# Sliding windows by DMA alone: 11 of 32 batches staged in SBUF and stored twice, the rest copied HBM to HBM, on two rings

## The chip, the core and the metric

The kernel runs on one core of one Trainium2 chip. The metric is the device time of one execution in microseconds (us). Data lives in HBM, the chip's main memory; SBUF is the core's on-chip memory of 128 partitions. Copies are made by 16 DMA engines. A DMA is issued by the queue of an engine: SP (`nc.sync`) or ACT (`nc.scalar`); each of the two has a hardware ring of its own. A DMA is broken into packets, one for each contiguous run of memory.

## The reference: what is computed

Nothing is computed; overlapping windows are copied. The input is fp32 of shape (32, 4096, 256), the output (32, 127, 64, 256).

```python
window_size = 64
stride = 32
n_windows = (length - window_size) // stride + 1      # 127
for i in range(n_windows):
    start = i * stride
    result[:, i] = x[:, start:start + window_size].copy()
```

A window is 64 rows of 256 floats, 65,536 bytes, and contiguous both in the input and in the output. Windows advance by half a window. Call 32 rows (32,768 bytes) a block: a batch has 128 blocks, and window i is blocks i and i + 1. So every block but the first and the last of a batch is written twice. The input has 134.2 MB, the output 266.3 MB.

## The kernel before

The file holds five strategies; line 8 picks `"d2d"`, and only `_d2d` (line 33) and `_d2d_batch` (line 14) run. `_SbufBatch`, `_sbuf`, `_mix`, `_pair` and `_hybrid` are not used, and SBUF holds no data.

`_d2d` loops over the 32 batches. `D2D_NQ` is 1 (line 30), so all DMAs are issued on `nc.sync`. For each batch `_d2d_batch` issues two DMAs from HBM to HBM at line 26: one of 112 windows (`D2D_CHUNK`, line 11) and one of the remaining 15. Both sides of each are rows of 65,536 bytes, one for each window; the rows of the source overlap by half. There are 64 DMAs in all. No DMA depends on another; the Tile framework hands each a semaphore and lets the queue wait for an older one where semaphores run out. The order of the work is the order of issue, batch after batch. In the profile, line 283 is the start of the program, line 297 its end.

Of the kernel before, what the change touches and what calls it, by code (L numbers as in the profile page):

```python
# [7 lines left out]
STRATEGY = "d2d"  # L8
NSB = 7

D2D_CHUNK = 112


def _d2d_batch(q, x, out_flat, b, L, D, W, S, n_win):
    win_elems = W * D
    step_elems = S * D
    w0 = 0
    while w0 < n_win:
        nw = min(D2D_CHUNK, n_win - w0)
        src = bass.AP(  # L20
            x.tensor,
            x.offset + (b * L + w0 * S) * D,
            [[step_elems, nw], [1, win_elems]],
        )
        dst = out_flat[b * n_win + w0 : b * n_win + w0 + nw]
        q.dma_start(out=dst, in_=src, max_dma_last_dim=65536)
        w0 += nw


D2D_NQ = 1  # L30


def _d2d(nc, x, out, B, L, D, W, S, n_win):
    out_flat = out.rearrange("b i w d -> (b i) (w d)")
    queues = [nc.sync, nc.scalar][:D2D_NQ]
    for b in range(B):
        _d2d_batch(queues[b % len(queues)], x, out_flat, b, L, D, W, S, n_win)


class _SbufBatch:  # L40

    def __init__(self, tc, ctx, x, out, B, L, D, W, S, n_win, bufs=3):
        assert W % S == 0 and L % S == 0
        self.m = W // S
        self.n_blocks = L // S
        assert self.n_blocks <= 128
        self.blk = S * D
        self.n_win = n_win
        self.x_blocks = x.rearrange("b (n s) d -> b n (s d)", n=self.n_blocks)
        self.out_rows = out.rearrange("b i w d -> b i (w d)")  # L50
        self.pool = ctx.enter_context(tc.tile_pool(name="swin_sbuf", bufs=bufs))
        self.dtype = x.dtype
        self.chunks = []
        w0 = 0
        for cnt in (64, 48, 16, 15):
            while n_win - w0 >= cnt or (w0 < n_win and cnt == 15):
                cnt_eff = min(cnt, n_win - w0)
                self.chunks.append((w0, cnt_eff))
                w0 += cnt_eff
        assert sum(c for _, c in self.chunks) == n_win  # L60

    def alloc(self):
        return self.pool.tile([self.n_blocks, self.blk], self.dtype, name="xb")

    def load(self, q, t, b):
        q.dma_start(out=t[:, :], in_=self.x_blocks[b])

    def stores(self, q, t, b):
        for k in range(self.m):
            for (w0, cnt) in self.chunks:  # L70
                src = t[w0 + k : w0 + k + cnt]
                dst = self.out_rows[b, w0 : w0 + cnt, k * self.blk : (k + 1) * self.blk]
                q.dma_start(out=dst, in_=src, max_dma_last_dim=65536)


def _sbuf(ctx, tc, nc, x, out, B, L, D, W, S, n_win):
    sb = _SbufBatch(tc, ctx, x, out, B, L, D, W, S, n_win, bufs=4)
    queues = [nc.sync, nc.scalar]
    tiles = {}
    for b in range(B):  # L80
        t = sb.alloc()
        tiles[b] = t
        sb.load(queues[b % 2], t, b)
        if b >= 1:
            sb.stores(queues[(b - 1) % 2], tiles[b - 1], b - 1)
            del tiles[b - 1]
    sb.stores(queues[(B - 1) % 2], tiles[B - 1], B - 1)


def _mix(ctx, tc, nc, x, out, B, L, D, W, S, n_win, nsb=None, lookahead=2):  # L90
    if nsb is None:
        nsb = NSB
    out_flat = out.rearrange("b i w d -> (b i) (w d)")
    sb = _SbufBatch(tc, ctx, x, out, B, L, D, W, S, n_win, bufs=4)
    queues = [nc.sync, nc.scalar]

    span = B - 4
    sbuf_set = set()
    if nsb > 0:
        for j in range(nsb):  # L100
            sbuf_set.add(1 + j * span // nsb)
    assert len(sbuf_set) == nsb

    def flush_stores(qidx):
        t, bb = pending.pop(0)
        j = 0
        for (w0, cnt) in sb.chunks:
            for k in range(sb.m):
                q = queues[(qidx + j) % 2]
                src = t[w0 + k : w0 + k + cnt]  # L110
                dst = sb.out_rows[bb, w0 : w0 + cnt, k * sb.blk : (k + 1) * sb.blk]
                q.dma_start(out=dst, in_=src, max_dma_last_dim=65536)
                j += 1

    pending = []
    n_d2d_left = B - nsb
    for b in range(B):
        q = queues[b % 2]
        if b in sbuf_set:
            t = sb.alloc()  # L120
            sb.load(q, t, b)
            pending.append((t, b))
            if len(pending) > lookahead:
                flush_stores(b % 2)
        else:
            _d2d_batch(q, x, out_flat, b, L, D, W, S, n_win)
            n_d2d_left -= 1
            if pending and n_d2d_left < 2 * len(pending):
                flush_stores(b % 2)
    qi = 0  # L130
    while pending:
        flush_stores(qi)
        qi += 1


def _pair(ctx, tc, nc, x, out, B, L, D, W, S, n_win, nsb=None):
    if nsb is None:
        nsb = NSB
    assert 3 * nsb + 4 <= B - nsb, "not enough d2d batches to pair"
    out_flat = out.rearrange("b i w d -> (b i) (w d)")  # L140
    sb = _SbufBatch(tc, ctx, x, out, B, L, D, W, S, n_win, bufs=4)
    queues = [nc.sync, nc.scalar]
    blk = sb.blk

    sbuf_batches = [4 * g for g in range(nsb)]
    d2d_batches = [b for b in range(B) if b not in set(sbuf_batches)]
    di = 0

    W_CHUNKS = [(0, 64), (64, 48), (112, 15)]
    L_CHUNKS = [(0, 64), (64, 48), (112, 16)]  # L150

    def d2d_chunk(q, b, w0, cnt):
        src = bass.AP(
            x.tensor,
            x.offset + (b * L + w0 * S) * D,
            [[S * D, cnt], [1, W * D]],
        )
        q.dma_start(
            out=out_flat[b * n_win + w0 : b * n_win + w0 + cnt],
            in_=src,  # L160
            max_dma_last_dim=65536,
        )

    def load_part(q, t, b, p0, cnt):
        q.dma_start(out=t[p0 : p0 + cnt], in_=sb.x_blocks[b, p0 : p0 + cnt])

    def store_part(q, t, b, w0, cnt, k):
        src = t[w0 + k : w0 + k + cnt]
        dst = sb.out_rows[b, w0 : w0 + cnt, k * blk : (k + 1) * blk]
        q.dma_start(out=dst, in_=src, max_dma_last_dim=65536)  # L170

    tiles = {}
    n_groups = nsb + 2
    for g in range(n_groups):
        qa = queues[g % 2]
        qb = queues[1 - g % 2]
        a_instrs = []
        if g < nsb:
            bload = sbuf_batches[g]
            t = sb.alloc()  # L180
            tiles[bload] = t
            for (p0, cnt) in L_CHUNKS:
                a_instrs.append(("load", t, bload, p0, cnt, None))
        if g >= 2:
            bst = sbuf_batches[g - 2]
            ts = tiles.pop(bst)
            for (w0, cnt) in W_CHUNKS:
                for k in range(sb.m):
                    a_instrs.append(("store", ts, bst, w0, cnt, k))
        b_needed = [ins[4] for ins in a_instrs]  # L190
        b_instrs = []
        nb_d2d = 3 if g < nsb else 2
        for _ in range(nb_d2d):
            bd = d2d_batches[di]
            di += 1
            for (w0, cnt) in W_CHUNKS:
                b_instrs.append((bd, w0, cnt))
        n = max(len(a_instrs), len(b_instrs))
        for i in range(n):
            if i < len(a_instrs):  # L200
                ins = a_instrs[i]
                if ins[0] == "load":
                    load_part(qa, ins[1], ins[2], ins[3], ins[4])
                else:
                    store_part(qa, ins[1], ins[2], ins[3], ins[4], ins[5])
            if i < len(b_instrs):
                bd, w0, cnt = b_instrs[i]
                d2d_chunk(qb, bd, w0, cnt)
    rem = d2d_batches[di:]
    for j, bd in enumerate(rem):  # L210
        for (w0, cnt) in W_CHUNKS:
            d2d_chunk(queues[j % 2], bd, w0, cnt)


def _hybrid(ctx, tc, nc, x, out, B, L, D, W, S, n_win):
    out_flat = out.rearrange("b i w d -> (b i) (w d)")
    sb = _SbufBatch(tc, ctx, x, out, B, L, D, W, S, n_win, bufs=3)

    sbuf_batches = [b for b in range(B) if (b + 1) * NSB // B > b * NSB // B]
# [16 lines left out]
    if pending is not None:  # L236
        sb.stores(q_sb, pending[0], pending[1])
# [64 lines left out]
```

## Time and profile before

| | |
|---|---|
| time, median of 2 runs | 807.83 us (807.09 to 808.56) |
| span of the profiled execution | 805.2 us |
| instructions | 109, of which 64 issue DMAs |
| bytes moved by DMA | 266.34 MB, mean 331 GB/s |
| HBM read and written | 266.34 MB each |
| one DMA, from issue to landing, median | 100.5 us |

The profiled execution's own time is its span; the three numbers of the first row come from other, unprofiled executions. In the page, section 2 cuts the span into 40 slices; its DMA row is the mean busy share of the 16 engines in tenths, and GB/s what they moved. A byte copied from HBM to HBM counts once in the GB/s of the engines, and twice in the HBM traffic (read and written). Section 3 gives the packets of each queue. The view by stretches gives, for a window of time, its length, the busy time of POOL, the clock, the DMA share and the GB/s; the share times 16 is the number of engines at work on average. The view of the waits of a queue gives for each line what it waited for: total us, times, longest.

### The profile page before, as it was taken

How to read it: one execution, taken by the hardware profiler on the slowest of the kernel's cores; microseconds unless marked ns; L12 is line 12 of the kernel's file. 1: busy time of each engine (PE TensorE's matmuls, PEld its weight loads, DVE VectorE, ACT ScalarE, POOL GpSimd, SP SyncE). 2: the span in 40 equal slices, each digit the busy share in tenths (PEclk: the TensorE clock that was granted, in tenths of full speed). 3: DMA queues.
4: the chain of work that ended last, by engine and by line, in shares of the span. 5: the costliest groups of instructions: out<-in, count | busy, mean ns of one | idle time of the engine just before them, and what ended most of it. 6: DMA issues, size and time to landing. Idle time of an engine off the chain costs nothing. (4 is left out here: it accounts for less than half of the span.)

```text
span 805.2 us, 109 instructions
## 1 busy us (share of the span) xinstructions
POOL 0.2 (0%) x4
## 2 busy tenths in 40 slices
POOL 0000000000000000000000000000000000000000
DMA  9999999999999999999999999999999999999995
GB/s 313 355 322 332 342 316 352 322 339 335 319 358 313 322 352 319 348 329 335 339 316 358 319 329 348 313 361 319 335 335 332 342 322 339 332 322 332 326 335 254
DMA packets 5056, 266.34 MB, mean 331 GB/s; under 512 B 992, under 2 KB 992, under 8 KB 992
## 3 DMA queue, kind: packets, MB, share of 16 engines
q1 hardware_dynamic: 5056, 266.34, 98.3%
HBM read 266.34 MB, written 266.34 MB: 662 GB/s over the span
## 5 line engine op out<-in xcount | busy, mean ns | idle before, releaser
L283 POOL MEMSET const-bfloat16-1.0<- 128x1 bf16 x1 | 0.1, 101 | 0.0
L283 POOL MEMSET const-uint8-127<- 128x1 uint8 x1 | 0.1, 101 | 0.0
L283 POOL MEMSET const-float32-0.0<- 128x1 f32 x1 | 0.1, 98 | 0.2 <-issue 0.2
L283 POOL MEMSET const-float32-1.0<- 128x1 f32 x1 | 0.1, 98 | 0.0
## 6 DMA issues: line engine op xcount, KB each, us to landing
out_dram<-in_x_dram SPq DMA_DIRECT2D x64, 100.5
```

Of the source, the lines that this page charges most:

```text
L283: nc = _bacc.Bacc("TRN2", target_bir_lowering=False, num_devices=1)
```

## The change

The five strategies go, and a class `Copier` with four kinds of DMA comes. 11 batches (1, 4, 7, ... 31) are staged: `load` brings a whole batch, 128 blocks, into an SBUF tile, one block for each partition, and four `store` calls write it out: blocks 0 to 126 as the first halves of the windows (`half` 0), blocks 1 to 127 as the second halves, each in a part of 112 rows and one of 15. The other 21 batches go from HBM to HBM: `d2d` for 112 windows as before, and `d2d_fine` for the last 15, whose rows are cut into 16 runs of 4096 bytes, with the 16 as the outer dimension.

Work goes in 11 groups. Group g stages one batch on one ring (`qa`) and copies two direct batches on the other (`qb`); the rings change roles from group to group. The load of a batch is issued two groups ahead, on the ring that will store it; the pool has four tiles. The last group has one direct batch left. There are 97 DMAs: 11 loads, 44 stores, 21 of `d2d` and 21 of `d2d_fine`.

```diff
-STRATEGY = "d2d"
-NSB = 7
...
+class Copier:
...
+    def d2d(self, q, b, w0, n):
+        blk = self.blk
         q.dma_start(
+            out=self.oap((b * self.nw + w0) * 2 * blk, [[2 * blk, n], [1, 2 * blk]]),
+            in_=self.xap(b * self.nb + w0, [[blk, n], [1, 2 * blk]]),
             max_dma_last_dim=65536,
         )
+    def d2d_fine(self, q, b, w0, n, parts=16):
+        blk = self.blk
+        e = 2 * blk // parts
+        q.dma_start(
+            out=self.oap((b * self.nw + w0) * 2 * blk, [[e, parts], [2 * blk, n], [1, e]]),
+            in_=self.xap(b * self.nb + w0, [[e, parts], [blk, n], [1, e]]),
+        )
+    def load(self, q, t, b):
+        q.dma_start(
+            out=t[:, :], in_=self.xap(b * self.nb, [[self.blk, self.nb], [1, self.blk]])
+        )
+    def store(self, q, t, b, half, p0, n):
+        blk = self.blk
+        w = b * self.nw + p0 - half
+        q.dma_start(
+            out=self.oap(w * 2 * blk + half * blk, [[2 * blk, n], [1, blk]]),
+            in_=t[p0 : p0 + n, :],
+        )
...
-    if STRATEGY == "d2d":
-        _d2d(nc, x, out, B, L, D, W, S, n_win)
...
+    c = Copier(nc, x, out, B, L, D, W, S, n_win)
+    pool = ctx.enter_context(tc.tile_pool(name="xb", bufs=4))
+    rings = [nc.sync, nc.scalar]
+    staged = list(range(1, B, 3))
+    direct = [b for b in range(B) if b not in staged]
+    tiles = {}
+    def load(q, g):
+        if g < len(staged):
+            tiles[g] = pool.tile([128, c.blk], x.dtype, name="xb")
+            c.load(q, tiles[g], staged[g])
+    load(rings[0], 0)
+    load(rings[1], 1)
+    for g, b in enumerate(staged):
+        qa, qb = rings[g % 2], rings[1 - g % 2]
+        load(qa, g + 2)
+        t = tiles.pop(g)
+        for half in (0, 1):
+            if direct:
+                d = direct.pop(0)
+                c.d2d(qb, d, 0, 112)
+                c.d2d_fine(qb, d, 112, 15)
+            c.store(qa, t, b, half, half, 112)
+            c.store(qa, t, b, half, 112 + half, 15)
+    for d in direct:
+        c.d2d(rings[d % 2], d, 0, 112)
+        c.d2d_fine(rings[d % 2], d, 112, 15)
```

`xap` and `oap`, left out above, make an access pattern on the input and the output from a start and a list of [step, count]; `blk` is 8192 elements, `nb` 128, `nw` 127.

More of the change, by code (lines that the diff above doesn't have):

```diff
@@ L4 @@
 import concourse.tile as tile
-from concourse import bass_utils, mybir
+from concourse import mybir
 from concourse._compat import with_exitstack
-STRATEGY = "d2d"
-NSB = 7
[L11 to L27, printed above, removed]
@@ L30 @@
[L30 to L46, printed above, removed]
-        self.blk = S * D
[L48 to L73, printed above, removed]
@@ L76, in _sbuf @@
[L76 to L133, printed above, removed]
@@ L136, in _pair @@
[L136 to L157, printed above, removed]
+BLK = 32 * 256
@@ new lines, with __init__, xap, oap @@
+class Copier:
+    def __init__(self, nc, x, out, B, L, D, W, S, n_win):
+        assert W == 2 * S and L % S == 0
+        self.nc, self.x, self.out = nc, x, out
+        self.blk = S * D
+        self.nb = L // S
+        self.nw = n_win
+    def xap(self, block, dims):
+        return bass.AP(self.x.tensor, self.x.offset + block * self.blk, dims)
+    def oap(self, elem, dims):
+        return bass.AP(self.out.tensor, self.out.offset + elem, dims)
+    def d2d(self, q, b, w0, n):
+        blk = self.blk
@@ L158, in d2d_chunk @@
         q.dma_start(
-            out=out_flat[b * n_win + w0 : b * n_win + w0 + cnt],
-            in_=src,
+            out=self.oap((b * self.nw + w0) * 2 * blk, [[2 * blk, n], [1, 2 * blk]]),
+            in_=self.xap(b * self.nb + w0, [[blk, n], [1, 2 * blk]]),
             max_dma_last_dim=65536,
         )
[L164 to L219, printed above, removed]
-    d2d_batches = [b for b in range(B) if b not in set(sbuf_batches)]
-    q_d2d = nc.sync
-    q_sb = nc.scalar
-    pending = None
-    prefetch = None
-    for b in range(B):
-        if b in set(d2d_batches):
-            _d2d_batch(q_d2d, x, out_flat, b, L, D, W, S, n_win)
-        else:
-            t = sb.alloc()
-            sb.load(q_sb, t, b)
-            if pending is not None:
-                sb.stores(q_sb, pending[0], pending[1])
-            pending = (t, b)
-    if pending is not None:
-        sb.stores(q_sb, pending[0], pending[1])
+    def d2d_fine(self, q, b, w0, n, parts=16):
[5 more added lines that the diff above has]
+        )
@@ L249 @@
     nc = tc.nc
-    W = int(window_size)
-    S = int(stride)
+    W, S = int(window_size), int(stride)
     B, L, D = x.shape
     n_win = (L - W) // S + 1
-    assert out.shape == (B, n_win, W, D), (out.shape, (B, n_win, W, D))
-    if STRATEGY == "d2d":
-        _d2d(nc, x, out, B, L, D, W, S, n_win)
-    elif STRATEGY == "sbuf":
-        _sbuf(ctx, tc, nc, x, out, B, L, D, W, S, n_win)
-    elif STRATEGY == "mix":
-        _mix(ctx, tc, nc, x, out, B, L, D, W, S, n_win)
-    elif STRATEGY == "pair":
-        _pair(ctx, tc, nc, x, out, B, L, D, W, S, n_win)
-    else:
-        _hybrid(ctx, tc, nc, x, out, B, L, D, W, S, n_win)
+    assert out.shape == (B, n_win, W, D)
+    c = Copier(nc, x, out, B, L, D, W, S, n_win)
[24 more added lines that the diff above has]
+        c.d2d_fine(rings[d % 2], d, 112, 15)
 _INS = ['x', 'window_size', 'stride']
```

## The prediction

> **What bounds the kernel now.** I read the page first. Compute does nothing (POOL 0.2 us in all), so the chain of work that ended last says nothing here, and the DMA rows carry the case.
>
> ```profile
> DMA  9999999999999999999999999999999999999995
> DMA packets 5056, 266.34 MB, mean 331 GB/s; under 512 B 992, under 2 KB 992, under 8 KB 992
> q1 hardware_dynamic: 5056, 266.34, 98.3%
> HBM read 266.34 MB, written 266.34 MB: 662 GB/s over the span
> ```
>
> The 16 DMA engines are busy 98.3% of the span. 5056 less 992 is 4064 packets, one of 65,536 B for each window (32 x 127). The 992 small ones are 32 x (16 + 15): a DMA of 112 windows signs off on 16 engines, one of 15 windows on 15. Every byte crosses HBM twice, once read and once written.
>
> Next, the waits of the SP queue and the issuing line, to see if the issuer starves the engines.
>
> ```profile
> SPq L26 <- DMA out_dram<-in_x_dram: 662.8, 56, 21.6
> ```
> ```profile
> L26 SPq DMA_DIRECT2D out_dram<-in_x_dram x64: 528/748/927, 0.7 to 707.6; - x64
> DMA to landing us min/median/max: 24.6/100.5/101.9
> ```
>
> SP issues 64 DMAs at a median of 748 ns and waits 56 times: all but the first eight wait for an older one, so at most eight are in flight. A DMA lands 100.5 us after its issue, mostly queued behind others. The last is issued at 707.6 us. The issuer is far ahead and bounds nothing.
>
> Busy engines are not yet a bound: they may be held up together. The view of busy time by stretch decides (DMA share and GB/s are the last two columns).
>
> ```profile
> 20.00:700.00 680.00, 0.00 (x0) 1.00 1.00 334
> 745.00:780.00 35.00, 0.00 (x0) 1.00 0.94 331
> 790.00:800.00 10.00, 0.00 (x0) 1.00 0.73 315
> ```
>
> With all 16 busy they move 334 GB/s, 20.9 each (3.14 us per packet). At 0.94, some 15 engines move 331, 22.0 each. At 0.73, 11.7 engines move 315, 27.0 each (2.43 us per packet). A quarter of the engines gone costs 6% of the rate. So an engine alone can do at least 27.0, together 16 x 27.0 = 432 GB/s, and something shared stops direct copies at about 334. The likeliest shared thing is HBM traffic, 2 x 334 = 668 GB/s of reads and writes.
>
> **The change, part by part.** All sums are against the profiled execution: span 805.2 us, 2.6 below the median of the two runs (807.83), which I add at the end. At 334 GB/s the 266.34 MB take 797.4 us; the other 7.8 us are the start and the thinning end.
>
> *Traffic.* A batch has 8.32 MB of output and 4.19 MB of input. Direct, the engines move 8.32 MB and HBM carries 16.65. Staged, the engines move 4.19 in and 8.32 out, 12.52 MB, and HBM carries the same 12.52. With 11 staged and 21 direct: engine bytes 266.34 + 11 x 4.19 = 312.5 MB (+17%); HBM traffic 532.7 - 11 x 4.13 = 487.3 MB (-8.5%), all of it fewer reads: 220.9 read, 266.3 written. It trades the scarce resource, if that is total HBM traffic, against one with slack.
>
> *Bounds.* If both ceilings were used perfectly: engines 312.5 / 432 = 723 us, HBM 487.3 / 668 = 729 us. The sum cannot be below 729 by these rows. If the kinds never helped each other, direct at 334 and staged at 432 one after the other: 174.8 / 334 + 137.7 / 432 = 523 + 319 = 842 us. Alone, a staged batch is dearer than a direct one (29.0 us against 24.9). The whole gain is that direct packets run faster beside staged ones. That is why both rings matter: in each group one ring carries staged work and the other two direct batches.
>
> *How they mix.* The trace has one ring, so how engines share two is not in it. I bound by two ways. (a) Equal bytes: 129.3 MB staged beside 129.3 direct; HBM would allow 668 / 1.5 = 445, engines stop at 432: 599 us. The two first loads, 8.4 MB alone, 19 us. The direct rest, 45.5 MB at 334, 136 us. Sum 754. (b) Packet by packet, 64 KB direct against 32 KB staged: 2 to 1 in bytes, so HBM stops the pair at 668 / (5/3) = 401 GB/s. 10.5 pairs of 8.32 + 16.65 MB, 262.2 MB, take 654 us; the remaining 50.3 MB staged face staged work or nothing at 432, 116 us. Sum 770. I take the middle, 762, since neither is shown.
>
> [...]
>
> *Staged packets.* No row shows a packet with an end in SBUF. Its rate lies between that of a direct packet under full load, 20.9 GB/s, and 27.0, the fastest engine shown (a faster one is possible, but HBM then binds). I take 27.0: the staged packet burdens HBM half as much, as the uncrowded engines of 790 to 800 us do. The lower end is a rival below.
>
> [...]
>
> *Packets.* Per engine the packets go from 316 to 823: 147 of 64 KB, 315 of 4 KB (the fine form of the 15-window tails), 88 loads, 176 stores, 97 sign-offs. The engine time outside packets is 1.7%, 13.7 us for 316, so at most 43 ns each; 507 more cost 0 to 22 us. I take 0, because the stretch from 20 to 700 us shows a share of 1.00: one packet's gap is covered by the next. The other ring is the cover; without it, 22.
> The fine form puts 15 windows on 16 engines evenly. The 15-row stores still use 15 engines, 22 packets of 32 KB less on one, 0.2% of the bytes. Worth 0 to 5 us of the 7.8 at the ends; I take nothing.
>
> *Issue and waits.* 97 DMAs (11 loads, 44 stores, 42 direct) over two queues at 0.75 us: some 37 us per queue, beside transfers. SP no longer issues alone; ACT, idle before, issues half. New waits: a load waits until the tile of four groups earlier is stored; behind it on its ring stand the four stores of its group. Those older stores left on the same ring two groups before, with 16.6 MB of direct work since (about 40 us), so they should be done. A store waits for a load issued two groups earlier. If a ring does stall, the other still feeds all 16 engines at 334 or more instead of 401, 1.7 us lost per 10 us. If the limit of eight in flight is shared by both rings, that is still nearly one group (26 MB, 65 us of work). I take 0; ten such stalls of 10 us would be 17.
> *Crowding.* In (b) engines run at 401 of 432 while HBM is full. The row at 0.94 lost 1% near such a corner; 0 to 3%, up to 20 us. Taken as 0.
>
> Sum: 762 + 7.8 + 2.6 = 773 us.
>
> **The rivals.**
> *Writes bind, not the total.* Reads and writes fell together in every row, so a limit of 334 on writes alone fits too. Writes stay 266.3 MB: 797 us, plus 19 for the two opening loads, when nothing is written, plus 10: 827 us; 808 if the opening costs nothing. Against: nothing but that total traffic is the simpler reading.
> *Direct packets stay slow (the slower side).* Place: the 64 KB packet on an engine that alternates. If 3.14 us is what any 16-engine crowd costs a direct packet, staging only adds: 842 + 10 = 853 us. Turning point: with staged packets at 27.0 (319 us per engine in all), the 167 direct packets of an engine have 797 - 319 = 478 us, 2.87 us each. Above that it is slower than before. For: every crowded stretch shows it. Against: 2.43 us at 0.73.
> *Staged packets are no faster than crowded direct ones.* All at 334: 312.5 / 334 + 10 = 946 us. The engines must average 312.5 / 797 = 392 GB/s, 24.5 each, to break even: 91% of the best shown, so there are only 9% to lose.
> *Nothing changes because the DMA is hidden* is excluded: DMA is the whole span.
>
> **How the numbers follow.** Forecast mechanism 0.68: 740 (perfect mixing, 729 + 10) to about 815 (unknown costs in full on (b)), its likely part 745 to 800. Of it 0.62 falls below 791.7, faster by over 2%, and 0.06 within. Writes bind 0.13: 0.08 within, 0.05 above 824. The two slower ones together 0.19. About 2% is what a measurement of this kernel can tell from no change. So faster 0.62, same 0.14, slower 0.24. The range runs from 740 to 830: it takes in the writes rival and leaves out the 0.19 above and a little below. The forecast's own range is 740 to 800.
>
> **What would show it.** The DMA rate should rise from 334 to some 400 to 430 GB/s while HBM traffic stays near 650 to 670: 312.5 MB of engine bytes, 220.9 read. Direct packets should last some 2.4 to 2.7 us in the mixed stretches; near 3.1 with staged ones at 1.2 means the second rival, staged ones at 1.6 the third. A rate in which writes stay at 334 means the first. Wrong also if the share falls well below 0.95 in the middle: then waits for tiles or the in-flight limit starve a ring. Stretches with 334 GB/s would be direct facing direct.

## The result and the profile after

The changed kernel takes 844.55 us (median of 2 runs) against 807.83 before: ratio 1.0462, 95% interval 1.0349 to 1.0576. A second measurement (e16 below) gave 1.0449 (1.0412 to 1.0486). It is slower; 773 us had been predicted, and a faster kernel. The profiled execution is the shorter of the two (840.94 us) and has a span of 839.2 us.

First the page of the changed kernel, the rows of DMA. q1 is the ring of SP, q10 that of ACT.

```profile
DMA  9999999999999999999999999999999999999984
GB/s 372 365 405 403 382 400 405 333 387 382 356 362 315 405 392 364 426 395 385 332 362 411 366 392 409 379 367 344 402 389 366 420 377 386 345 378 400 393 294 147
DMA packets 13124, 312.48 MB, mean 372 GB/s; under 512 B 1530, under 2 KB 1530, under 8 KB 6570
q1 hardware_dynamic: 6600, 158.34, 49.9%
q10 hardware_dynamic: 6524, 154.14, 48.2%
HBM read 220.92 MB, written 266.34 MB: 581 GB/s over the span
```

The change did what it says: 312.48 MB through the engines, 220.92 MB read, the rings balanced. The rate rose from 331 to 372 GB/s, but 392 were needed to break even. HBM traffic fell from 662 to 581 GB/s, well under the 668 that the prediction took as the ceiling. The engines look as busy as before (98.1%). So on average neither ceiling of the prediction was reached, 432 GB/s for the engines or 668 for HBM: the engines were busy, but slow.

The stretches of the same kernel (length, POOL, clock, DMA share, GB/s) show a shortfall from 432 everywhere and a thin end:

```profile
20.00:100.00 80.00, 0.00 (x0) 1.00 1.01 387
200.00:300.00 100.00, 0.00 (x0) 1.00 1.01 361
700.00:780.00 80.00, 0.00 (x0) 1.00 1.00 375
780.00:839.20 59.20, 0.00 (x0) 1.00 0.73 269
```

The mean hides three kinds of stretch. The DMA view of the changed kernel, narrowed to short windows, gives each ring's packets, MB and share of the 16 engines. From 90 to 105 us SP stores (32 KB packets) beside direct 64 KB packets on ACT:

```profile
DMA packets 127, 6.23 MB, mean 415 GB/s; under 512 B 0, under 2 KB 0, under 8 KB 0
q10 hardware_dynamic: 63, 4.13, 66.6%
q1 hardware_dynamic: 64, 2.10, 33.8%
```

63 packets against 64: one of each in turn, 415 GB/s. This is what the prediction hoped for. From 150 to 165 us ACT stores, and SP has a fine tail, 4 KB packets:

```profile
DMA packets 326, 5.16 MB, mean 344 GB/s; under 512 B 33, under 2 KB 33, under 8 KB 188
q10 hardware_dynamic: 166, 4.52, 94.9%
q1 hardware_dynamic: 160, 0.63, 10.3%
```

Again about one packet for one, but the direct ring gives 0.63 MB beside 4.52. The stores are almost alone, and they don't fill the engines' 432 GB/s either: 4.52 MB in 15 us is 301. From 250 to 270 us both rings carry direct work (without the sign-offs and 74 packets of 4 KB, 92 packets with 6.03 MB are left, 64 KB each), near the rate of the kernel before:

```profile
DMA packets 181, 6.33 MB, mean 317 GB/s; under 512 B 15, under 2 KB 15, under 8 KB 89
```

From the trace's packet records, the mean of a 64 KB packet is 2.68 us (3.11 before), of a load packet 1.30, of a store packet of the 112-row parts 1.46, of a 4 KB packet 0.18. More than half of those store packets take 1.21 us, as fast as any; the slowest tenth takes 2.26 us or more.

### The profile page after: what moved, and what is told of

It reads as the page before. It is cut to its first block, busy times and chain, and to the rows that moved or that the text cites. A ratio compares the mean times of both kernels' runs of the same rounds, so it can differ in the third digit from the quotient of the medians.

```text
span 839.2 us, 154 instructions
## 1 busy us (share of the span) xinstructions
POOL 0.2 (0%) x4
## 2 busy tenths in 40 slices
DMA packets 13124, 312.48 MB, mean 372 GB/s; under 512 B 1530, under 2 KB 1530, under 8 KB 6570
## 3 DMA queue, kind: packets, MB, share of 16 engines
HBM read 220.92 MB, written 266.34 MB: 581 GB/s over the span
```

## The experiments

Theory F ("fine"): the fine tails un-mix the rings, if an engine takes whole packets in turn, however small (e11 and e12 below measure the turns). Theory S ("store"): stores of 112 and 15 rows are slow for a reason on the SBUF side. Rivals: W, a limit on writes to HBM; small packets dear in themselves; the second ring.

### Each cost undone, alone and together

`e1_plain_tail` undoes the fine form:

```diff
-                c.d2d_fine(qb, d, 112, 15)
+                c.d2d(qb, d, 112, 15)
```

> The changed kernel, with the 15-window tails of the direct batches as 64 KB packets (one to an engine) in place of 16 x 15 packets of 4 KB. Theory F (an engine that takes one packet from each ring in turn moves only 4 KB of direct data beside each 32 KB staged packet while a fine tail is in its ring, 15 turns on end, so the two kinds are not mixed for some half of the span): the staged-alone stretches at 335 to 360 GB/s go, the time falls by 40 to 70 us, to 770 to 805. Rival S (the staged stores themselves are slow, 1.46 us mean against 1.21 at best, for a reason on the SBUF side): the tails matter little, 825 to 845 us, store packets stay at 1.45 to 1.6 us.

`e7_rows128_fine` undoes the store shape and keeps the fine tails, `e5_rows128_plain` undoes both. 127 is no multiple of the 16 engines, 128 is. So half 0 writes block 127 too, to the first half of the next batch's window 0, and half 1 writes block 0, to the last half window of the batch before. Those neighbours are direct batches; their 15-window tail, moved to the end that is overwritten, goes out two groups later. (Batch 31 has no successor and keeps 112 and 15 for half 0.)

```diff
-                c.d2d(qb, d, 0, 112)
-                c.d2d_fine(qb, d, 112, 15)
-            c.store(qa, t, b, half, half, 112)
-            c.store(qa, t, b, half, 112 + half, 15)
...
+                first = d % 3 == 2
+                c.d2d(qb, d, 15 if first else 0, 112)
+                late.append((g + 2, qb, d, 0 if first else 112))
...
+                c.store(qa, t, b, half, 0, 128)
```

Left out here: the function that issues what `late` holds, with `d2d_fine` in e7 and `d2d` in e5, and the exception for batch 31.

> Only the stores are mended (128 rows), the fine tails stay. Theory S as a cost of its own: the 2794 store packets of the changed kernel lose 1.47 - 1.22 us each, 44 us of each engine, so 840 falls to 795 to 810. If F is the whole cause: 830 to 845.

> Both suspected costs undone: plain 64 KB tails, and stores of 128 rows (half 0 also writes block 127 to the place of the next batch's first half window, half 1 block 0 to that of the batch before; the direct tails that put the right data there go out two groups later). Theories F and S together: store packets at 1.21 to 1.25 us, 791 less some 15 to 20 us, 770 to 780, near sum (b) of the prediction, which left both costs out. If the store shape does not matter in the mix: 790 to 797 as with plain tails alone; if the wait of the tails for the stores costs: above that.

The changed kernel again, and e5 again, on one chip:

> The changed kernel itself on the same chip: 1.04 to 1.05 of before.

> The kernel with 128-row stores, plain tails and 64 KB direct packets once more, for a comparison on one chip: 0.970 of before again.

| ratio to before (95% interval), us | fine tails | plain tails |
|---|---|---|
| stores of 112 + 15 rows | 1.0449 (1.0412 to 1.0486), 843.9 (e16) | 0.9852 (0.9834 to 0.9871), 793.3 (e1) |
| stores of 128 rows | 1.0097 (1.0076 to 1.0118), 815.3 (e7) | 0.9702 (0.9686 to 0.9718), 783.1 (e5) |

e14 repeated e5: 0.9707 (0.9689 to 0.9726). Both costs are there. F is the larger: 51 us with the stores as they are, 32 with good stores. S is 29 with fine tails, 10 with plain ones. Together 61. (The four ran on three chips; by the ratios the 51 are 48 and the 10 are 12.) F is the fine form alone in both rows. S as measured here holds one thing more than the row count: the later place of the tails.

e1 fell in the range of theory F. e7 came out 5 us over its range: S alone had been taken to give back all the store packets' loss. e5 lies 3 us over its own. It beats before by 3%.

The packet records, cut into pieces of 5 us and sorted by the most frequent packet of each ring, show how the two costs work together. Staged packets with no 64 KB packets on the other ring fill 410 us of the changed kernel, 380 of them beside a fine tail, at some 365 GB/s; in e7, with 128 rows, the stretches beside a fine tail run at 416. In e1 such time is 160 us, so slow stores matter less there. And staged work that runs without direct work leaves direct work to meet itself: both rings carry direct work for 205 us of the changed kernel and 235 of e7, at 290 to 355 GB/s, but for 20 us of e1 and 40 of e5.

### What the second ring and small packets cost by themselves

`e4_direct_two_rings` copies all 32 batches HBM to HBM, in turn on the two rings, with fine tails.

> No staging: all 32 batches go HBM to HBM, alternately on the two rings, with the fine tails. Tells what the second ring and the fine tails do by themselves. All theories: HBM traffic is the bound as before, 334 GB/s, 800 to 812 us; theory F costs nothing here, since a 4 KB packet beside a 64 KB one leaves HBM just as full. If small packets are dear in themselves (0.19 us where 0.15 is their share by bytes): up to 8 us more.

Measured 1.0065 (1.0040 to 1.0089), 810.4 us. Its 7680 packets of 4 KB, more than the 5040 of the changed kernel, and the second ring cost 5 us together. So small packets are cheap, and F is not their price but what they run beside.

### How an engine shares two rings

`e11_turns_4k` and `e12_turns_64k` hold only the part in question: the same 32 KB packets on SP, beside 4 KB or 64 KB ones on ACT; all else is left out.

> Measures how engines share two rings: 4 loads and 6 stores of 128 rows on SP (42 MB in 32 KB packets) beside two direct DMAs of 112 windows in 4 KB packets on ACT (14.7 MB); the rest of the work is left out. Theory F, packets in turn: about one 4 KB packet for each 32 KB packet while both have work, so direct data move at some 45 to 55 GB/s, staged at some 380. If rings share by bytes: 8 small packets for each large one, direct at some 200 GB/s.

> The same with direct packets of 64 KB. Packets in turn: as many 64 KB as 32 KB packets while both have work, direct at 267 and staged at 134 GB/s. Sharing by bytes: two 32 KB packets for each 64 KB one, some 210 GB/s each.

The DMA view of e11 from 15 to 75 us:

```profile
DMA packets 1516, 25.26 MB, mean 421 GB/s; under 512 B 80, under 2 KB 80, under 8 KB 840
q1 hardware_dynamic: 756, 22.15, 86.8%
q10 hardware_dynamic: 760, 3.11, 12.7%
```

And of e12 from 15 to 55 us:

```profile
q10 hardware_dynamic: 169, 10.03, 61.5%
q1 hardware_dynamic: 175, 5.21, 37.6%
```

760 packets against 756, and 169 against 175, sign-offs of DMAs included: turns go by packet, not by bytes. The 4 KB ring gets 3.11 MB in 60 us, 52 GB/s, the 64 KB ring 10.03 in 40 us, 251 GB/s. In the changed kernel a fine tail has 240 packets, 15 for each of 16 engines, 21 tails 315 turns. A tail of 64 KB packets has one, on 15 engines (e1 has 1509 sign-offs, 21 fewer than the 1530 of the changed kernel).

### Stores alone

Four tiles are loaded once; then only stores, on SP. The loop is that of e8 (`n` = 112) and e9 (`n` = 64); e3 has the same with 128. e2 goes batch by batch with the 112 and 15 rows of the changed kernel.

```diff
+    for i in range(B * n_win // n):
+        for half in (0, 1):
+            w = n * i
+            nc.sync.dma_start(
+                out=c.oap(w * 2 * c.blk + half * c.blk, [[2 * c.blk, n], [1, c.blk]]),
+                in_=tiles[i % 4][0:n, :],
+            )
```

> Leaves out all direct copies and all loads but four: four tiles are loaded once, and the stores of 32 batches go out from them in parts of 112 and 15 rows on one ring, 266.3 MB. Theory S: store packets at 1.55 us or more with nothing beside them, 330 GB/s or less, 805 us or more. Rival W (HBM takes writes at some 400 GB/s at most, the best written rate in a 20 us stretch of the changed kernel being 407): 1.3 us a packet, 660 to 680 us. If stores are only slow when mixed: 1.21 us, 432 GB/s, 630 us.

> As the stores alone, but in parts of 128 rows that take all 128 partitions and all 16 engines evenly (260 MB, the last 96 windows are left out and no window holds what it should). Theory S in the form that the 112 and 15 rows hit the SBUF unevenly: packets at 1.21 to 1.28 us, 410 to 430 GB/s, 620 to 650 us. If stores from SBUF, or writes to HBM, are slow whatever their rows: the same rate as with 112 and 15 rows.

> Stores alone in parts of 112 rows from partitions 0 to 111, 7 rows to an engine, 259.8 MB (no window holds what it should, the last 32 are left out). Tells how much of the 112 + 15 stores' loss (1.76 us a packet) the 112 rows have. If the 15 rows, which lie on neighbouring partitions, make the jam: 112 rows alone near 1.21 to 1.35 us, 650 to 720 us. If rows that 16 engines take in sevens meet at the same ways into the SBUF: 1.6 us or more, 850 us or more.

> Stores alone again, in parts of 64 rows from partitions 0 to 63, 4 rows to an engine, all 16 engines at work, 260.1 MB (no window holds what it should, the last 32 are left out). If stores are slow by the evenness over engines: 4 rows each is even, 1.21 us a packet, 640 to 650 us. If engines meet at shared ways into the SBUF that go by partition: slower than 128 rows. [...]

The views by stretch, well inside each run; 112 and 15 rows as in the changed kernel (e2):

```profile
100.00:900.00 800.00, 0.00 (x0) 1.00 0.94 280
```

128 rows (e3):

```profile
50.00:640.00 590.00, 0.00 (x0) 1.00 1.00 432
```

112 rows alone (e8):

```profile
100.00:800.00 700.00, 0.00 (x0) 1.00 0.98 297
```

64 rows (e9):

```profile
100.00:1300.00 1200.00, 0.00 (x0) 1.00 1.00 206
```

In whole runs 1026, 647, 962 and 1332 us for about the same bytes. 128 rows write 432 GB/s, so rival W is out: in e3 HBM has nothing but writes from 50 to 640 us, and they keep the 432 GB/s that the prediction took for 16 engines. The 112 rows themselves are slow, the 15 add little. 64 rows are 4 for each of 16 engines and are the slowest, with a share of 1.00 over 1200 us, so that all 16 are at work: it is not evenness over the engines. Nor do engines wait for work in e9: 99 in 100 of its packets take 2.48 to 2.57 us. In e3 nearly all take 1.21 to 1.23. In e8 some 40% take 1.21 to 1.22 and a tenth 2.57 or more: some packets are held up, the others are not.

What changes from e3 to e9 is which partitions are in use at once: all 128, or 0 to 63. Half the partitions went with half the rate: the 206 GB/s of e9 are 16 x 32.8 KB / 206 = 2.55 us a packet, against 1.21 in e3. So the second case of e9's expectation came, slower than 128 rows, 1332 us against 647. That engines meet at shared ways into the SBUF was the author's conjecture: no run shows such ways. 112 rows, at 297 of 432 GB/s, lose more than their share of rows, and no run shows why.

A rival was not tested by itself: with another row count the engines may also write to places in HBM that lie differently far apart. Against it for the 112 rows: the direct packets of e12 come from DMAs of 112 windows too, and last 2.42 us in the median, 27.1 GB/s. So the runs show that the rate goes with the row count of a store (206, 297 and 432 GB/s for 64, 112 and 128 rows), and leave open whether the SBUF side is the reason.

### What is left

`e6_eight_staged` (8 staged batches always on SP, 24 direct always on ACT) was to match packets in turn with bytes 1 to 2.

> 8 of 32 batches staged, always on SP, 24 direct, always on ACT, with 128-row stores and plain tails. If an engine takes packets in turn from its rings (32 KB staged, 64 KB direct), 8 staged batches have half the bytes of 24 direct ones, the two rings end together and nearly all is mixed at 401 GB/s: 299.9 MB in 748 us, 752 to 768 with the ends. If the rings share by bytes: staged work ends a third before the end, direct work goes on alone at 334 GB/s, 772 to 785. If the mix of kinds does not count, only the number staged: between 780 and 805.

Measured 0.9960 (0.9945 to 0.9975), 803.9 us: in the range of the third case, whose reason, that the mix does not count, its stretches contradict:

```profile
20.00:460.00 440.00, 0.00 (x0) 1.00 1.00 410
480.00:740.00 260.00, 0.00 (x0) 1.00 1.00 332
```

Until 460 us the rate was even above the 401 expected, but staged work was done at some 475 us, and direct work ran on alone. Packets in turn alone would not have let it get so far ahead. The trace shows why: ACT's fourth DMA waited until 63 us for a semaphore that a load of SP had taken at 1 us, its fifth until 105 us for that of a store of SP, and so on. For some 110 us of the first 475 the ACT ring had no data packets, or next to none.

`e10_direct_32k` is e5 with direct packets cut to 32 KB (`max_dma_last_dim=32768`); `e15_direct_32k` is the same again.

> The kernel with 128-row stores and plain tails, its direct packets cut to 32 KB in place of 64. If engines take packets in turn, direct and staged share by bytes, pairs run at up to 432 GB/s in place of 401: sum (a), 754 + 10, 762 to 776 us. If the order in which the rings get work decides the mix: 779 to 787, as with 64 KB. If more packets cost: above 787.

> The same with 32 KB direct packets once more, on the same chip: 0.960 of before, if its gain is not the chip's; 0.970 to 0.975 if it was.

Against before e10 gave 0.9605 (0.9588 to 0.9623), but on a chip where before took 819 us; e15, on the chip of e14, gave 0.9720 (0.9700 to 0.9740) against e14's 0.9707. So the gain of e10 was the chip's, and 32 KB packets bring none. `e13_matched` matches bytes and packet sizes: 13 staged batches on SP, 19 direct on ACT, all packets 32 KB, 128-row stores.

> 13 staged batches on SP and 19 direct ones on ACT, all packets 32 KB, 128-row stores, plain tails: 163.6 MB staged beside 158.1 MB direct, equal packets in turn, so that no direct work meets direct work. 321.7 MB at 432 GB/s are 745 us, with 10 for the ends 755; 750 to 768 if the two rings stay in step. If the eight DMAs in flight or the waits of stores for stores let one ring run dry: 770 to 800.

Measured 0.9795 (0.9770 to 0.9819), 790.8 us, the "run dry" case. Its stretches, and the DMA view from 350 to 395 us:

```profile
20.00:640.00 620.00, 0.00 (x0) 1.00 1.00 427
660.00:760.00 100.00, 0.00 (x0) 1.00 0.99 331
```
```profile
q1 hardware_dynamic: 604, 17.50, 90.5%
q10 hardware_dynamic: 90, 1.97, 10.1%
```

For 620 us it ran at 427 of 432 GB/s. But the ACT ring was nearly empty at times, and its work came last, alone, at 331. The trace tells why it was empty: both queues share the semaphores 99 to 106. SP took 104 and 99 for stores at 339 and 341 us; ACT's next DMAs waited for just those two and went out at 361 and 383, 15-window tails both. Its next large one waited until 405 for 102, which a load of SP had taken at 352. So the eight DMAs in flight are eight for both rings, and the ring that is ahead takes the other's places. No run gives each ring places of its own, so what the sharing costs in us is not measured.

## Why the prediction was wrong, point by point

- **Direct packets speed up beside staged ones: right. HBM traffic as the shared limit: it fits, by exclusion.** Well-mixed stretches run at 415, and the mean direct packet fell from 3.11 to 2.68 us, under the turning point of 2.87. So the rival with slow direct packets is out; that its 853 us lie near the measured time is chance. Writes alone are not the limit (432 GB/s written in e3), and neither are reads: from 15 to 55 us of e12 SP's packets are all loads, so the engines read 381 GB/s there (15.24 MB in 40 us). That total traffic stops at 668 is not shown by itself; mixed stretches carried up to some 650 over hundreds of us (e5, e1).
- **"Staged packets ... I take 27.0": wrong for stores.** It holds for 128 rows (432 GB/s, 27.0 for each engine) but not for parts of 112 and 15: 280 GB/s alone, 17.5 for each engine, below even the lower end of 20.9. That is the third rival's case, for these stores with little beside them: 1.65 us a packet from 150 to 165 us. Over the whole changed kernel they averaged 1.46 us, 22.4 GB/s. The bounds came from packets with both ends in HBM and could not contain that 17.5. The cost is 29 us with the fine tails, 10 once the tails are plain.
- **"Packets ... 0 to 22 us. I take 0": the step that failed most.** As a price of the packets it was right (e4, 5 us at most). But sum (b) rests on turns by packet, and was worked out as if all direct data came in 64 KB packets. The same turns give a 4 KB packet a place beside a 32 KB one, so for up to 315 turns of each engine staged work ran almost without direct work. "The other ring is the cover" was the error: it was the other ring that paid. 51 us with the stores as they are, 32 with good stores.
- **How two rings mix:** packets in turn, way (b), is shown (756 packets beside 760 in e11, 175 beside 169 in e12, 64 beside 63 in the changed kernel itself), so (b) was the one to take, not the middle of (a) and (b). The rate of 432 for equal packets is shown too (434 from 100 to 160 us of e13, with 447 packets of ACT beside 458 of SP).
- **Issue and waits, taken as 0:** the eight places are shared, and that has a part in which ring has work. In e6 and e13 it let staged work run ahead, and the direct work that was left ran alone, at 331 to 332 GB/s. The changed kernel shares them too: ACT's fifth DMA waited until 61 us for a semaphore that a direct copy of SP held. There it was not undone, so its part is open. Most of the direct work beside direct work, as at 250 to 270 us, went with the fine tails (205 us to 20 in e1).
- **The ends, 7.8 us: too small.** With both costs undone e5 has a span of 780.5 us against 770 predicted. Its end:

```profile
120.00:680.00 560.00, 0.00 (x0) 1.00 1.00 414
705.00:780.50 75.50, 0.00 (x0) 1.00 0.87 315
```

Its middle is faster than the 401 of (b). At 414 to the end the last 75.5 us would have been 57: 18 us, more than the whole difference of 10.5.

So the mixing of the two kinds held. Of the 72 us between 773 (the prediction's terms add up to 772) and 844.55, the two costs make 61; the kernel without them, at 783, lies 1.3% above the forecast. That nearness is partly luck: its middle was faster than (b), its end slower. What was wrong was to take two details of the change, the fine tail and the row counts, as free.

## What to carry to other kernels

When two streams share the engines, count turns, not bytes: where packets go one for one, as here, the stream with the small packets gives up its share (52 of 421 GB/s in e11), so don't cut one stream far smaller than the other: 4 KB beside 32 KB cost 51 us here, while 64 KB or 32 KB beside 32 KB made no difference (0.9707 of before in e14, 0.9720 in e15). Ask of every DMA that touches SBUF how many rows it has and on which partitions (stores of 64 and 128 rows ran at 206 and 432 GB/s here), and measure its shape alone before it stands in a sum. Staging part of a copy through SBUF gained 3% here at best; where one kind was left to run alone, much less (0.4% in e6).

## What had not been expected

Copies within HBM gained nothing from a second ring (810.4 us in e4), yet staged work, mostly with direct work beside it, reached 427 GB/s for 620 us (e13). Stores of 128 rows ran at 432 GB/s over 590 us, the fastest of the long stretches; 112 rows, an eighth fewer, at 297, and 64 rows at 206. The eight semaphores of DMAs are shared by both queues, so that rings with different work hold each other up at the issue, with nothing to be seen in the busy share (1.00 in e6 and e13).
